# Merging two of the three products of a weight tile where there are 256 tokens

## The chip, the cores and the metric

The kernel runs on one core of a Trainium2 chip. TensorE (PE) multiplies, with its weight loader (PEld) beside it; VectorE (DVE), ScalarE (ACT) and GpSimd (POOL) do elementwise work; SyncE (SP) issues the loads of the weights. The metric is device time in microseconds for one execution. The kernel before took 2243.93 us, the median of three runs (2242.37 to 2246.74).

## The reference

A network in float32 over 256 tokens with 1024 features, preceded by 16 meta tokens (272 rows in all). The first block is a mixer (a state-space part and a conformer convolution, joined by one output product) and a mixture of experts; the second block has two layers, each a feed-forward part, an attention and a feed-forward part. The expert layer has 16384 experts with one row each; a token uses 16 of them for each of 8 heads:

```
h = h + concatenate([y_ssd, y_conf]) @ w_out
q = (xt @ w_query).reshape(t, 8, 256)
expert_idx, gate = top 16 of the sums of the two halves' scores
act = gelu(einsum("td,thkd->thk", xt, w_down[idx])) * gate
h = h + einsum("thk,thkd->td", act, w_up[idx])
...
ffn(x) = (silu(x @ wi_a) * (x @ wi_b)) @ wo
```

The meta tokens don't take part in the expert layer, and from the second layer's attention output on they are not needed either: there products have 256 columns, one per token, elsewhere mostly 272.

## The kernel before

Features stand on the partitions and tokens on the free axis. All large weights come in one stream, in the order of use, in chunks of eight 128x128 tiles. `_split` turns half a chunk (four tiles, 128x512) into two parts of TensorE's faster float32 type: ACT writes the first part H (L288, "wH"), then DVE or POOL the remainder L = w - H (L294, "wL"); the number `share` sets how many of the remainders go to POOL (0.5, every second one, in the down rows). The activations are cut in the same way, into uH and uL, cH and cL, gH and gL. `wtile` hands out a tile, and lets splits run up to four half chunks ahead.

`mm3` computes one tile of a product with three products into one PSUM bank: H by xH (L315), H by xL (L316), L by xH (L317). `linear` walks over the output tiles, each with its own bank (three "mm" banks at the expert layer), and calls `evac` with the sum; `linear_cut` interleaves the first few output tiles. `pair` does two outputs together, for the feed-forward part's input. All are used in every stage but one, the "up" product of the experts, which has a loop of its own (L999).

The stages with 256 columns that the change is about: the mixer's output product w_out (16 sums, L649, DVE adds each to h); the experts' query (16 tiles, L835 multiplies by the norm's factor, then the scores L840 and the search for the 16 best on DVE); the down product (`peer`, 128 rows of 8 tiles, each row 128 experts by 256 tokens, closed by a Gelu on ACT in `value`, L957); the second attention's output (`proj_out`); and the last feed-forward part's output (L1093).

All experts are computed, as a dense product, and the gates of those not chosen are zero. The gates are built beside the down product. The choice of experts (`route`, a generator) is issued in steps between the rows, `pace` 1.5 steps a row: its dense part runs over 128x864 elements in L894, L895 and L897 on DVE. From row 60 on the gates are made four tokens at a time: `onehot` (L931, L933 and, on ACT, L936) writes one-hot rows, `gates` turns them into gates with eight passes of TensorE (L943) and multiplies (L945). The order on each engine is the order in which the program was written down by the scheduler; an engine works it off in that order.

## Time and profile before

| | |
|---|---|
| median of three runs | 2243.93 us |
| span of the profiled execution | 2244.9 us |
| TensorE busy | 2174.1 us (97%), 17351 instructions |
| weight loader busy | 2100.5 us (94%) |
| VectorE busy | 1587.7 us (71%) |
| ScalarE busy | 1322.5 us (59%) |
| GpSimd busy | 672.5 us (30%) |
| traffic | 356.59 MB, 159 GB/s on average |

The profile is of one execution, and its own time is the span; little lies around it, as the run's first and last records are a load and a store. A "busy" matmul counts from its start to a modelled end, so that neighbouring ones overlap; distances between starts are the better measure. "a <- b" in a row of waits says that a waited for b. The stages on the timeline, by the first product of each: w_out 193.5 to 255 us, query to 308.4, down to 762 (its rows 60 to 127 from 508.7), up to 1128, the second block to the end, whose last stage, from about 2178 on, is the last feed-forward part's output.

### The profile page before, as it was taken

The page shows a single profiled execution, that of the slowest core. Times are in us where ns is not written, and L with a number is a line of the kernel's source. Part 1 is how long each engine was busy: PE and PEld are TensorE (multiplying, and loading weights), DVE is VectorE, ACT ScalarE, POOL GpSimd, SP SyncE. Part 2 cuts the span into 40 slices and gives each one's busy share as a digit, 9 for nine tenths or more (in the row PEclk, how much of TensorE's full clock was granted, in tenths as well). Part 3 has the DMA queues.
Part 4 walks back from the last instruction along what each step waited for, and adds up shares of the span by engine and source line. Part 5 has one row for each costly group of instructions (what it writes and reads, how often), then busy time and mean ns, then how long its engine had stood idle before and what let it go on. Part 6 is the DMA issues. An engine that isn't in the chain of part 4 may idle for free.

```text
span 2244.9 us, 45779 instructions
## 1 busy us (share of the span) xinstructions
PE 2174.1 (97%) x17351; PEld 2100.5 (94%) x17351; DVE 1587.7 (71%) x3143; ACT 1322.5 (59%) x2857; POOL 672.5 (30%) x567
## 2 busy tenths in 40 slices
PE   8998998899999999999999999999999999899999
PEld 7987997899999999999999998899999999679999
DVE  8899789946778765666586655876656666877664
ACT  8776654556766655555555555765555555656553
POOL 6685744444555300000031123122201212412220
PEclk9999999999999999999999999999999999999999
DMA  4534644454444555555565554145555555204554
GB/s 169 166 104 132 201 142 149 159 181 150 142 135 139 186 185 185 188 186 183 186 199 192 178 169 133 65 152 170 178 179 170 172 178 178 76 29 141 183 188 157
DMA packets 103948, 356.59 MB, mean 159 GB/s; under 512 B 12416, under 2 KB 20016, under 8 KB 103344
## 3 DMA queue, kind: packets, MB, share of 16 engines
q1 hardware_dynamic: 100096, 346.06, 46.6%
q10 hardware_dynamic: 3632, 7.62, 1.0%
q8 instruction: 136, 2.23, 0.4%
q14 instruction: 84, 0.69, 0.1%
HBM read 351.51 MB, written 5.40 MB: 159 GB/s over the span
## 4 chain that ended last, share of the span: by engine, by line
PE 77%; DVE 14%; ACT 4%; issue 3%; POOL 1%; DMA 1%; SPq 0%; DVEq 0%; ACTq 0%; POOLq 0%
PE acc L999 16%; PE mm L315 14%; PE mm L317 14%; PE mm L316 14%; PE acc L317 4%; PE acc L316 4%; PE acc L315 4%; DVE wL L294 3%; DVE h L931 2%; DVE acc L526 1%; ACT h L936 1%; PE acc L943 1%; PE mm L1458 1%; ACT wH L288 1%; PE acc L1482 1%
## 5 line engine op out<-in xcount | busy, mean ns | idle before, releaser
L288 ACT ACTIVATE wH<-raw 128x512 fp32r<-128x512 f32 x1296 | 806.3, 629 | 565.0 <-PE mm L316 251.5
L294 DVE TENSOR_TENSOR wL<-raw,wH 128x512 fp32r<-128x512 f32 x1037 | 757.1, 731 | 388.5 <-ACT wH L288 369.0
L317 PE MATMUL mm<-uH,wL 128*128 128x256 f32 (+1 forms) x2168 | 619.6, 286 | 21.8 <-DVE wL L294 20.8
L315 PE MATMUL mm<-uH,wH 128*128 128x256 f32 (+1 forms) x2168 | 627.6, 290 | 9.9 <-ACT wH L288 6.9
L316 PE MATMUL mm<-uL,wH 128*128 128x256 f32 (+1 forms) x2168 | 618.9, 285 | 2.2 <-DVE uL L359 2.0
L294 POOL TENSOR_TENSOR wL<-raw,wH 128x512 fp32r<-128x512 f32 x259 | 384.1, 1488 | 462.6 <-ACT wH L288 357.9
L317 PEld LDWEIGHTS mm<-uH,wL 128*128 128x128 f32 x2168 | 410.3, 189 | 27.1 <-DVE wL L294 26.2
L315 PEld LDWEIGHTS mm<-uH,wH 128*128 128x128 f32 x2168 | 410.3, 189 | 15.5 <-ACT wH L288 8.7
L316 PEld LDWEIGHTS mm<-uL,wH 128*128 128x128 f32 x2168 | 410.0, 189 | 5.7 <-DVE uL L359 4.0
L999 PE MATMUL acc<-uH,wH 128*128 128x256 f32 x1024 | 288.4, 282 | 2.7 <-ACT uH L355 1.6
L999 PE MATMUL acc<-uL,wH 128*128 128x256 f32 x1024 | 287.7, 281 | 0.4 <-DVE uL L357 0.4
L999 PE MATMUL acc<-uH,wL 128*128 128x256 f32 x1024 | 287.2, 281 | 0.0
L1083 POOL TENSOR_TENSOR t<-t,g 128x272 f32<-128x272 f32 (+1 forms) x88 | 108.4, 1233 | 416.7 <-ACT wH L288 320.5
L317 PE MATMUL acc<-uH,wL 128*128 128x272 f32 (+1 forms) x728 | 209.3, 288 | 0.0
L316 PE MATMUL acc<-uL,wH 128*128 128x272 f32 (+1 forms) x728 | 209.0, 287 | 0.0
L315 PE MATMUL acc<-uH,wH 128*128 128x272 f32 (+1 forms) x728 | 208.9, 287 | 0.0
L315 PE MATMUL mm<-gH,wH 128*128 128x272 f32 (+1 forms) x704 | 201.9, 287 | 0.0
L317 PE MATMUL mm<-gH,wL 128*128 128x272 f32 (+1 forms) x704 | 201.7, 286 | 0.0
L316 PE MATMUL mm<-gL,wH 128*128 128x272 f32 (+1 forms) x704 | 201.5, 286 | 0.0
L999 PEld LDWEIGHTS acc<-uH,wH 128*128 128x128 f32 x1024 | 194.1, 190 | 3.4 <-ACT uH L355 1.8
L999 PEld LDWEIGHTS acc<-uL,wH 128*128 128x128 f32 x1024 | 193.1, 189 | 0.6 <-DVE uL L357 0.6
L999 PEld LDWEIGHTS acc<-uH,wL 128*128 128x128 f32 x1024 | 193.1, 189 | 0.0
(400 smaller groups left out, 3914.1 us busy)
## 6 DMA issues: line engine op xcount, KB each, us to landing
raw<-in_wall_dram SPq DMA_DIRECT2D x648, 512.0 KB, 3.3
bdram<-brow ACTq DMA_DIRECT2D x1, 3200.0 KB, 13.9
b<-bdram SPq DMA_DIRECT2D x8, 272.0 KB, 5.3
b<-bdram SPq DMA_DIRECT2D x8, 144.0 KB, 3.7
buf<-in_keys_dram ACTq DMA_DIRECT2D x1, 1024.0 KB, 7.1
hd<-h ACTq DMA_DIRECT2D x1, 1024.0 KB, 5.3
h<-hd ACTq DMA_DIRECT2D x1, 1024.0 KB, 7.5
uv<-in_uv_dram ACTq DMA_DIRECT2D x1, 1024.0 KB, 5.9
```

Source lines behind the costliest of these rows:

```text
L288: nc.scalar.activation(out=H, in_=w, func=AF.Copy)
L294: eng.tensor_tensor(out=L, in0=w, in1=H.bitcast(F32), op=ALU.subtract)
L315: mm(ps, H, xH, start=(k == 0), stop=False)
L316: mm(ps, H, xL, start=False, stop=False)
L317: mm(ps, L, xH, start=False, stop=(k == kt - 1))
L526: nc.vector.scalar_tensor_tensor(out=acc, in0=src, scalar=w, in1=acc, op0=ALU.mult, op1=ALU.add)
L931: nc.vector.tensor_tensor(out=o, in0=self.iota[:, None, None, :].to_broadcast([P, 4, 2, P]), in1=sel[:, ts, :, None].to_broadcast([P, 4, 2 ...
L936: nc.scalar.activation(out=o[:, t, 0], in_=o[:, t, 0], func=AF.Copy, scale=gsel[:, 4 * g + t : 4 * g + t + 1])
L943: nc.tensor.matmul(ps[:, :, t], o[:, t, 1], o[:, t, 0], start=True, stop=True)
L999: nc.tensor.matmul(o, a, b, start=(r == 0 and d % 2 == 0 and i == 0), stop=(r == NT - 1 and i == 2), skip_group_check=True)
L1083: nc.gpsimd.tensor_tensor(out=t, in0=t, in1=s, op=ALU.mult)
L1458: nc.tensor.matmul(ps[:, :nk], qa[hh][:, k, a : a + n], ckv[:, k, :nk], start=(k == 0), stop=(k == 1))
```

## The change

Both parts of the rows are kept in one tile, [partition, feature block, part, token]: uu, nn, cc, gg, oo, qp. Where a product has 256 tokens and is called with `wide=True`, its result takes a full bank as two halves of 256: H meets both parts in one 512-column product (first half xH, second half xL), and L meets xH in a 256-column product into the first half. The halves are added afterwards. `add_to` (w_out, the second attention's output) adds both halves to h, one after the other on DVE. `whole` (query, down rows) copies one half to SBUF on ACT and adds the other on DVE. The last feed-forward part's output does its scaled sum twice. The up product and all 272-column products keep three products a tile.

```diff
-        self.uH = per.tile([P, KD, T], F32R, name="uH")
-        self.uL = per.tile([P, KD, T], F32R, name="uL")
+        self.uu = per.tile([P, KD, 2, T], F32R, name="uu")
+        self.uH, self.uL = self.uu[:, :, 0], self.uu[:, :, 1]
...
     def mm3(self, ps, x, kt, a=0, b=None):
         mm = self.nc.tensor.matmul
         for k in range(a, kt if b is None else b):
             H, L = self.wtile()
-            xH, xL = x(k)
-            mm(ps, H, xH, start=(k == 0), stop=False)
-            mm(ps, H, xL, start=False, stop=False)
-            mm(ps, L, xH, start=False, stop=(k == kt - 1))
+            xx = x(k)
+            if len(ps.shape) == 3:
+                mm(ps, H, xx, start=(k == 0), stop=False)
+                mm(ps[:, 0], L, xx[:, 0], start=False, stop=(k == kt - 1))
+            else:
+                mm(ps, H, xx[:, 0], start=(k == 0), stop=False)
+                mm(ps, H, xx[:, 1], start=False, stop=False)
+                mm(ps, L, xx[:, 0], start=False, stop=(k == kt - 1))
...
+    def result(self, n, wide, tag="mm"):
+        ps = self.bank(tag)
+        return ps.rearrange("p (w n) -> p w n", w=2) if wide else ps[:, :n]
+    def linear(self, mt, kt, x, n, evac, tags=("mm",), wide=False):
         for m in range(mt):
-            ps = self.bank(tags[m % len(tags)])[:, :n]
+            ps = self.result(n, wide, tags[m % len(tags)])
             self.mm3(ps, x, kt)
             self.flush()
             evac(m, ps)
 
-    def linear_cut(self, mt, kt, at, x, n, evac):
-        ps = [self.bank()[:, :n] for _ in range(CUT)]
+    def linear_cut(self, mt, kt, at, x, n, evac, wide=False):
+        ps = [self.result(n, wide) for _ in range(CUT)]
         for m in range(CUT):
             self.mm3(ps[m], x, kt, 0, at)
         for m in range(CUT):
             self.mm3(ps[m], x, kt, at, kt)
             evac(m, ps[m])
-        self.linear(mt - CUT, kt, x, n, lambda m, p: evac(m + CUT, p))
+        self.linear(mt - CUT, kt, x, n, lambda m, p: evac(m + CUT, p), wide=wide)
+    def add_to(self, o, ps):
+        for i in range(2):
+            self.nc.vector.tensor_tensor(out=o, in0=ps[:, i], in1=o, op=ALU.add)
+    def whole(self, ps):
+        t = self.t_("sq", 3)[:, :S]
+        self.nc.scalar.activation(out=t, in_=ps[:, 1], func=AF.Copy)
+        self.nc.vector.tensor_tensor(out=t, in0=ps[:, 0], in1=t, op=ALU.add)
+        return t
 
...
-        return lambda k: (self.uH[:, k, a:b], self.uL[:, k, a:b])
+        return lambda k: self.uu[:, k, :, a:b]
...
-            cH = pool.tile([P, KD, S], F32R, name="cH")
-            cL = pool.tile([P, KD, S], F32R, name="cL")
+            cc = pool.tile([P, KD, 2, S], F32R, name="cc")
+            cH, cL = cc[:, :, 0], cc[:, :, 1]
...
-                nc.vector.tensor_tensor(out=h[:, m, M:], in0=ps, in1=h[:, m, M:], op=ALU.add)
-            self.linear_cut(8, KD, 4, lambda k: (yH[:, k], yL[:, k]), S, add)
+                self.add_to(h[:, m, M:], ps)
+            self.linear_cut(8, KD, 4, self.u(M, T), S, add, wide=True)
...
-            self.linear(8, KD, lambda k: (cH[:, k], cL[:, k]), S, add2)
+            self.linear(8, KD, lambda k: cc[:, k], S, add2, wide=True)
...
-                nc.vector.tensor_tensor(out=q, in0=ps, in1=r, op=ALU.mult)
+                nc.vector.tensor_tensor(out=q, in0=self.whole(ps), in1=r, op=ALU.mult)
...
-            self.linear(16, KD, self.u(M, T), S, qf)
+            self.linear(16, KD, self.u(M, T), S, qf, wide=True)
...
             def value(r, ps):
                 n = 4 * done
+                ps = self.whole(ps)
                 if n < S:
...
-                self.linear(1, KD, self.u(M, T), S, lambda m, ps: value(r_, ps))
+                self.linear(1, KD, self.u(M, T), S, lambda m, ps: value(r_, ps), wide=True)
...
-            gH = pool.tile([P, KF, n], F32R, name="gH")
-            gL = pool.tile([P, KF, n], F32R, name="gL")
+            gg = pool.tile([P, KF, 2, n], F32R, name="gg")
+            gH, gL = gg[:, :, 0], gg[:, :, 1]
...
-                nc.vector.scalar_tensor_tensor(out=self.h[:, m, lo:], in0=ps, scalar=0.5, in1=self.h[:, m, lo:], op0=ALU.mult, op1=ALU.add)
+                for p in (ps[:, 0], ps[:, 1]) if lo else (ps,):
+                    nc.vector.scalar_tensor_tensor(out=self.h[:, m, lo:], in0=p, scalar=0.5, in1=self.h[:, m, lo:], op0=ALU.mult, op1=ALU.add)
...
-            self.linear(8, KF, lambda k: (gH[:, k], gL[:, k]), n, add)
-    def proj_out(self, oH, oL, nxt, lo=0):
+            self.linear(8, KF, lambda k: gg[:, k], n, add, wide=lo > 0)
...
         self.norm_begin(nxt, lo)
 
         def add(m, ps):
-            self.nc.vector.tensor_tensor(out=self.h[:, m, lo:], in0=ps, in1=self.h[:, m, lo:], op=ALU.add)
+            if lo:
+                self.add_to(self.h[:, m, lo:], ps)
+            else:
+                self.nc.vector.tensor_tensor(out=self.h[:, m], in0=ps, in1=self.h[:, m], op=ALU.add)
             self.norm_tile(m)
 
-        self.linear_cut(8, KD, 6, lambda k: (oH[:, k], oL[:, k]), T - lo, add)
+        self.linear_cut(8, KD, 6, lambda k: oo[:, k], T - lo, add, wide=lo > 0)
```

On TensorE, in a late row of the down product (banks mm, halves of chunks wH and wL, the gates' acc), before:

```order
L943 MATMUL acc_8501<-h_77 128x128 x4
L315 MATMUL mm_8510<-uH_78,wH_8430 128x256
L316 MATMUL mm_8510<-uL_79,wH_8430 128x256
L317 MATMUL mm_8510<-uH_78,wL_8431 128x256
L315 MATMUL mm_8510<-uH_78,wH_8430 128x256
L316 MATMUL mm_8510<-uL_79,wH_8430 128x256
L317 MATMUL mm_8510<-uH_78,wL_8431 128x256
L315 MATMUL mm_8510<-uH_78,wH_8430 128x256
L316 MATMUL mm_8510<-uL_79,wH_8430 128x256
L317 MATMUL mm_8510<-uH_78,wL_8431 128x256
```

and of the change:

```order
L965 MATMUL acc_6939<-h_77 128x128 x4
L318 MATMUL mm_6951<-uu_78,wH_6877 128x512
L319 MATMUL mm_6951<-uu_78,wL_6878 128x256
L318 MATMUL mm_6951<-uu_78,wH_6877 128x512
L319 MATMUL mm_6951<-uu_78,wL_6878 128x256
L318 MATMUL mm_6951<-uu_78,wH_6877 128x512
L319 MATMUL mm_6951<-uu_78,wL_6878 128x256
L318 MATMUL mm_6951<-uu_78,wH_6877 128x512
L319 MATMUL mm_6951<-uu_78,wL_6878 128x256
L318 MATMUL mm_6951<-uu_78,wH_6908 128x512
```

A weight tile has two rows now, and the row of experts keeps its place beside the gates' products.

On DVE, the last part of the routing's dense steps (buf) between the splits of the weights (wL), before:

```order
L897 TENSOR_REDUCE buf<-buf 128x16
L894 TENSOR_TENSOR buf<-buf,cst 128x864
L294 TENSOR_TENSOR wL<-raw,wH 128x512
L895 TENSOR_TENSOR buf<-buf 128x864
L894 TENSOR_TENSOR buf<-buf,cst 128x864
L897 TENSOR_REDUCE buf<-buf 128x16
L294 TENSOR_TENSOR wL<-raw,wH 128x512
L895 TENSOR_TENSOR buf<-buf 128x864
L894 TENSOR_TENSOR buf<-buf,cst 128x864
L294 TENSOR_TENSOR wL<-raw,wH 128x512
L897 TENSOR_REDUCE buf<-buf 128x16
L895 TENSOR_TENSOR buf<-buf 128x864
```

and of the change, where L916, L917 and L919 are the three lines that were L894, L895 and L897:

```order
L363 TENSOR_TENSOR sq<-mm,sq 128x256
L294 TENSOR_TENSOR wL<-raw,wH 128x512
L919 TENSOR_REDUCE buf<-buf 128x16
L294 TENSOR_TENSOR wL<-raw,wH 128x512
L363 TENSOR_TENSOR sq<-mm,sq 128x256
L916 TENSOR_TENSOR buf<-buf,cst 128x864 x2
L294 TENSOR_TENSOR wL<-raw,wH 128x512
L363 TENSOR_TENSOR sq<-mm,sq 128x256
L917 TENSOR_TENSOR buf<-buf 128x864 x2
L363 TENSOR_TENSOR sq<-mm,sq 128x256
L294 TENSOR_TENSOR wL<-raw,wH 128x512
L919 TENSOR_REDUCE buf<-buf 128x16 x2
```

The sum of the two halves (L363) comes once per row, and the same three lines stand among more splits than before.

On DVE, where the gates begin (one-hots h, gates' product acc, values buf), before:

```order
L294 TENSOR_TENSOR wL_6449<-raw_6430,wH_6448 128x512
L294 TENSOR_TENSOR wL_6485<-raw_6466,wH_6484 128x512
L294 TENSOR_TENSOR wL_6523<-raw_6504,wH_6522 128x512
L294 TENSOR_TENSOR wL_6571<-raw_6552,wH_6570 128x512
L945 TENSOR_TENSOR buf_3273<-acc_6539,buf_3273 128x62x4
L931 TENSOR_TENSOR h_77<-cst_68,sel_3275 128x1024
L961 TENSOR_TENSOR buf_3273<-t_6587,buf_3273 128x4
L945 TENSOR_TENSOR buf_3273<-acc_6590,buf_3273 128x63x4
L294 TENSOR_TENSOR wL_6622<-raw_6603,wH_6621 128x512
L931 TENSOR_TENSOR h_77<-cst_68,sel_3275 128x1024
L945 TENSOR_TENSOR buf_3273<-acc_6641,buf_3273 128x64x4
```

and of the change (L953 was L931, L967 was L945, L984 was L961):

```order
L294 TENSOR_TENSOR wL_6062<-raw_6047,wH_6061 128x512
L363 TENSOR_TENSOR sq_6030<-mm_6003,sq_6030 128x256
L953 TENSOR_TENSOR h_77<-cst_68,sel_3160 128x1024
L967 TENSOR_TENSOR buf_3158<-acc_6034,buf_3158 128x62x4
L363 TENSOR_TENSOR sq_6073<-mm_6046,sq_6073 128x256
L953 TENSOR_TENSOR h_77<-cst_68,sel_3160 128x1024
L984 TENSOR_TENSOR buf_3158<-t_6077,buf_3158 128x4
L967 TENSOR_TENSOR buf_3158<-acc_6080,buf_3158 128x63x4
L294 TENSOR_TENSOR wL_6108<-raw_6093,wH_6107 128x512
L363 TENSOR_TENSOR sq_6119<-mm_6092,sq_6119 128x256
L953 TENSOR_TENSOR h_77<-cst_68,sel_3160 128x1024
L967 TENSOR_TENSOR buf_3158<-acc_6126,buf_3158 128x64x4
```

One sum per row stands between the one-hots, the gates' multiplication and the splits.

## Rows read from the trace of the kernel before

**Rows 1.** The page: span, busy times, chain by engine and line, a costly group
```profile
span 2244.9 us, 45779 instructions
...
PE 2174.1 (97%) x17351; PEld 2100.5 (94%) x17351; DVE 1587.7 (71%) x3143; ACT 1322.5 (59%) x2857; POOL 672.5 (30%) x567
...
PE 77%; DVE 14%; ACT 4%; issue 3%; POOL 1%; DMA 1%; SPq 0%; DVEq 0%; ACTq 0%; POOLq 0%
PE acc L999 16%; PE mm L315 14%; PE mm L317 14%; PE mm L316 14%; PE acc L317 4%; PE acc L316 4%; PE acc L315 4%; DVE wL L294 3%; DVE h L931 2%; DVE acc L526 1%; ACT h L936 1%; PE acc L943 1%; PE mm L1458 1%; ACT wH L288 1%; PE acc L1482 1%
...
L294 DVE TENSOR_TENSOR wL<-raw,wH 128x512 fp32r<-128x512 f32 x1037 | 757.1, 731 | 388.5 <-ACT wH L288 369.0
```

**Rows 2.** Windows: stretch, length, busy us of PE, PEld, DVE, ACT, POOL; PEclk
```profile
193.50:230.00 36.50, 34.22 (x240) 30.38 (x238) 31.50 (x65) 24.39 (x52) 16.14 (x14) 1.00 0.34 112
255.00:308.40 53.40, 52.77 (x447) 52.57 (x447) 42.11 (x140) 27.31 (x53) 32.70 (x26) 1.00 0.64 210
308.40:463.00 154.60, 132.22 (x1066) 127.23 (x1066) 151.06 (x432) 75.34 (x149) 67.99 (x45) 1.00 0.45 147
463.00:508.70 45.70, 45.70 (x389) 45.70 (x388) 13.48 (x19) 24.32 (x48) 20.81 (x17) 1.00 0.59 191
508.70:657.00 148.30, 148.30 (x1273) 148.30 (x1272) 103.93 (x143) 101.53 (x305) 75.19 (x58) 1.00 0.42 141
657.00:762.00 105.00, 103.46 (x875) 102.40 (x874) 82.01 (x100) 67.37 (x215) 56.75 (x42) 1.00 0.47 153
```

**Rows 3.** PE's waits, 308.4 to 463 us: total us, times, longest
```profile
PE mm L317 <- DVE wL L294: 20.0, 19, 3.0
```

**Rows 4.** DVE's groups, 308.4 to 463 us: busy us, mean ns, idle before
```profile
L294 DVE TENSOR_TENSOR wL<-raw,wH 128x512 fp32r<-128x512 f32 x44 | 42.8, 976 | 2.2 <-ACT wH L288 2.2
```

**Rows 5.** Windows, PE alone: stretch, length, busy (instructions under way), PEclk
```profile
466.00:500.00 34.00, 34.00 (x290) 1.00 0.59 193
1500.00:1600.00 100.00, 100.00 (x795) 1.00 0.53 175
```

**Rows 6.** Timeline of PE, two streams: start us, us, instruction
```profile
252.72 0.28 PE L315 MATMUL mm<-cH,wH 128*128 128x256 f32 x1
...
253.63 0.28 PE L317 MATMUL mm<-cH,wL 128*128 128x256 f32 x1
...
2237.77 0.28 PE L317 MATMUL mm<-gH,wL 128*128 128x256 f32 x1
...
2241.01 0.28 PE L317 MATMUL mm<-gH,wL 128*128 128x256 f32 x1
```

**Rows 7.** Line L1450: ns min/median/max, first and last start us
```profile
L1450 PE MATMUL mm<-uv,ckv x24: 591/592/592, 1946.4 to 1956.3; 128*72 128x512 f32 x16, 128*128 128x512 f32 x8
```

**Rows 8.** Timeline of DVE around one sum of w_out
```profile
208.01 0.42 DVE L649 TENSOR_TENSOR h<-mm,h 128x256 f32<-128x256 f32 x1 [0.20 <-PE mm L317]
208.35 1.01 DVE L526 SCALAR_TENSOR_TENSOR acc<-cin,vecs,acc 128x256 f32<-128x256 f32 x2
```

**Rows 9.** ACT's groups, 465 to 505 us
```profile
L957 ACT ACTIVATE buf<-mm 128x256 f32<-128x256 f32 x14 | 5.1, 365 | 0.0
```

**Rows 10.** Timeline: query's start, first down rows, the end; [idle before <-releaser]
```profile
255.32 0.35 PE L315 MATMUL mm<-uH,wH 128*128 128x256 f32 x1 [1.41 <-DVE h L649]
...
311.13 0.39 PE L315 MATMUL mm<-uH,wH 128*128 128x256 f32 x1 [0.67 <-ACT uH L355]
...
2241.69 0.42 DVE L1093 SCALAR_TENSOR_TENSOR h<-mm,h 128x256 f32<-128x256 f32 x1 [5.96 <-PE mm L317]
```

**Rows 11.** PE's waits, 508.7 to 762 us
```profile
PE acc L943 <- DVE h L933: 0.2, 1, 0.2
```

**Rows 12.** DVE's groups, 657 to 745 us
```profile
L931 DVE TENSOR_TENSOR h<-cst,sel 128x1024 f32<-128x1024 f32 x24 | 31.2, 1299 | 0.0
```

**Rows 13.** L316's loads, 465 to 505 and 1500 to 1600 us: ns min/median/max
```profile
L316 PEld LDWEIGHTS mm<-uL,wH x112: 187/188/192, 465.1 to 504.8; 128*128 128x128 f32 x112
...
L316 PEld LDWEIGHTS mm<-uL,wH x136: 188/188/189, 1499.9 to 1599.4; 128*128 128x128 f32 x136
```

More of the change, by code (lines that the diff above doesn't have):

```diff
@@ L326, in flush @@
                 f()
-    def linear(self, mt, kt, x, n, evac, tags=("mm",)):
+    def result(self, n, wide, tag="mm"):
+        ps = self.bank(tag)
+        return ps.rearrange("p (w n) -> p w n", w=2) if wide else ps[:, :n]
+    def linear(self, mt, kt, x, n, evac, tags=("mm",), wide=False):
         for m in range(mt):
-            ps = self.bank(tags[m % len(tags)])[:, :n]
+            ps = self.result(n, wide, tags[m % len(tags)])
             self.mm3(ps, x, kt)
@@ L466, in mixer @@
             NU = 2
-            nH = pool.tile([P, KD, T], F32R, name="nH")
-            nL = pool.tile([P, KD, T], F32R, name="nL")
-            un = lambda a=0, b=T: lambda k: (nH[:, k, a:b], nL[:, k, a:b])
+            nn = pool.tile([P, KD, 2, T], F32R, name="nn")
+            nH, nL = nn[:, :, 0], nn[:, :, 1]
+            un = lambda a=0, b=T: lambda k: nn[:, k, :, a:b]
             r = None
@@ L1097, in add, with proj_out @@
                     nc.sync.dma_start(out=self.out[:, m], in_=self.h[:, m, M:])
-            self.linear(8, KF, lambda k: (gH[:, k], gL[:, k]), n, add)
-    def proj_out(self, oH, oL, nxt, lo=0):
+            self.linear(8, KF, lambda k: gg[:, k], n, add, wide=lo > 0)
+    def proj_out(self, oo, nxt, lo=0):
         self.norm_begin(nxt, lo)
         def add(m, ps):
-            self.nc.vector.tensor_tensor(out=self.h[:, m, lo:], in0=ps, in1=self.h[:, m, lo:], op=ALU.add)
+            if lo:
+                self.add_to(self.h[:, m, lo:], ps)
+            else:
+                self.nc.vector.tensor_tensor(out=self.h[:, m], in0=ps, in1=self.h[:, m], op=ALU.add)
             self.norm_tile(m)
-        self.linear_cut(8, KD, 6, lambda k: (oH[:, k], oL[:, k]), T - lo, add)
+        self.linear_cut(8, KD, 6, lambda k: oo[:, k], T - lo, add, wide=lo > 0)
     QT = ((0, M, M), (M, P, 144), (144, P, T))
@@ L1205, in attn_a @@
             rq = self.token_root(pool, pq, 16, 1.0 / 64, 0.125)
-            oH = pool.tile([P, 8, T], F32R, name="oH")
-            oL = pool.tile([P, 8, T], F32R, name="oL")
+            oo = pool.tile([P, 8, 2, T], F32R, name="oo")
+            oH, oL = oo[:, :, 0], oo[:, :, 1]
             def tail(items):
@@ L1285, in attn_a @@
                     tail([(1, 6, 2), (2, 6, 2)])
-            self.proj_out(oH, oL, nxt)
+            self.proj_out(oo, nxt)
     def meta_p(self, pool, qq, kz, rq, nlam):
@@ L1326, in attn_b @@
             cq = pool.tile([P, 2, T], F32, name="cq")
-            qH = pool.tile([P, 2, T], F32R, name="qH")
-            qL = pool.tile([P, 2, T], F32R, name="qL")
+            qp = pool.tile([P, 2, 2, T], F32R, name="qp")
+            qH, qL = qp[:, :, 0], qp[:, :, 1]
             kix = pool.tile([P, 2, T], F32, name="kix")
@@ L1332, in attn_b @@
             vt = pool.tile([P, 3, 1024], F32, name="vt")
-            oH = pool.tile([P, 8, S], F32R, name="oH")
-            oL = pool.tile([P, 8, S], F32R, name="oL")
+            oo = pool.tile([P, 8, 2, S], F32R, name="oo")
+            oH, oL = oo[:, :, 0], oo[:, :, 1]
             r = None
@@ L1386, in qif @@
                 nc.scalar.activation(out=qi[:, m], in_=ps, func=AF.Copy)
-            cqx = lambda k: (qH[:, k], qL[:, k])
+            cqx = lambda k: qp[:, k]
             self.linear(4, 2, cqx, T, qif)
@@ L1504, in attn_b @@
                 rq = rnext
-            self.proj_out(oH, oL, nxt, M)
+            self.proj_out(oo, nxt, M)
     def second(self):
```

## The prediction

> **What bounds the kernel now.** I read the page first. The profiled execution spans 2244.9 us, its TensorE (PE) is busy 97%, its weight loader 94%, VectorE (DVE) 71% [rows 1]. Busy PE is no proof that PE is the bound, so the chain of work that ended last comes second: PE holds 77% of it, DVE 14%, and among its lines stand the three products of a weight tile with 14% each and, with 3% DVE's split of the weights (L294) [rows 1]. So the matmul stream sets most of the time, and somewhere DVE does. The busy times by stage, third, say where. From 308.4 to 463 us, the first part of the experts' down product, DVE is busy 151.06 of 154.6 us and PE 132.22; the waits of that stretch are PE for DVE's split, 20.0 us in 19 waits [rows 2, 3]. There DVE is the bound. From 463 to 508.7 and to 657 PE is busy all of the time, DVE 13.48 of 45.7 and 103.93 of 148.3 us; to 657–762 DVE has 82.01 of 105 [rows 2]. In the query (255 to 308.4) PE has 52.77 of 53.4 us.
>
> **The price of a product.** Today a 128x128 weight tile costs three 256-column products. Between 466 and 500 us 290 of them are under way in 34.0 us without a gap, two of them from before its start, so 118 ns each; with 272 columns it is 795 in 100 us, 126 ns [rows 5]. The clock granted there is full (1.00), 2.4 GHz, at which a column takes 0.417 ns, if one goes in per cycle: 256 columns 106.7 ns. So each product carries some 11 ns more than its columns. How much depends on the tile that is read: with cH and cL eight products take 252.72 to 253.63, 114 ns each; with gH and gL 27 take 2237.77 to 2241.01, 120 ns [rows 6]. Both have 256 columns. An extra that is 7 ns with one tile and 13 with another, at one count of columns, looks like something paid where a product starts on its rows rather than a rate per column. Against this: 126 over 118 is 1.07 and 272 over 256 is 1.0625, which a rate per column gives too. I can't exclude it.
>
> No 512-column product of this number type is in the trace. Bounds from the nearest rows, per weight tile, of now 355 ns (3 x 118.3):
> - The extra goes with the columns: 512 columns cost two of 256, the tile stays at 355 ns, gain 0.
> - The extra is paid once per product: one of three goes, gain 11.6 ns.
> - The extra vanishes in a long product: the plain fp32 passes of L1450, also 512 columns, start 24 times from 1946.4 to 1956.3 us, 23 intervals of 430 ns; two cycles a column would be 426.7 [rows 7]. With as little as that, some 3 ns, a product would take 216, the tile 216 + 118, gain 20.8 ns.
> - Below nothing: a jump inside a product, from the first part's row to the second's, could cost as much as a start and something more; the spread of 114 to 120 between tiles puts that at 3 ns per tile, a loss.
>
> I take the second, 11.6 ns.
>
> **The change part by part.** 1520 weight tiles merge two products into one: 128 of w_out, 128 of the query, 1024 of the 128 down rows, 64 of the second attention's output, 176 of the last feed-forward part. The 272-column products and the "up" stage (L999) stay. But 384 of the 1024 tiles stand in the 48 down rows where DVE is the bound; PE's gain is lost there. That leaves 1136 x 11.6 ns = 13.2 us off the path.
>
> What is added, in the order of the program:
> - w_out, 16 tiles: a second DVE add each. DVE's add from PSUM with 128x256 takes 0.42 us and the next starts 0.34 after it [rows 8]. DVE is busy 31.50 of 36.5 us in 193.5 to 230 [rows 2]; 8 x 0.34 = 2.7 us if none of it is covered, 0 if the 5 idle us take it. I take 1. At the turn to the query PE waits 1.41 us for this very add (255.32) [rows 10]: +0.34.
> - Query, 16 tiles: ACT copies one half (0.365 us, by L957, the same shape out of PSUM [rows 9]), DVE adds. Both have room (DVE 42.11 of 53.4). +0.5, for 0 to 1. At its end PE waits for uL's sources (311.13) [rows 10]; copy and add stand ahead, 0.37 + 0.34 = 0.7.
> - Down rows under DVE's bound. One would charge 48 adds x 0.34 = 16 us. The order on DVE says otherwise: the steps of the routing (three passes over 128x864) are issued at a set pace, and between the last query row and the last of these steps stood 41 splits of the weights; now 48 splits and 47 adds. The DVE-bound stretch is thus 7 rows longer. A split takes DVE 0.98 us there [rows 4], of which I count 0.9, since the next instruction starts before the end as after the add. The stretch's end moves by 7 x 0.9 + 47 x 0.34 = 22.3 us, from 463 to some 485. But these are not lost: at 463 16 rows stood before row 60 (45.7 us of 24 x 118.3 ns, 2.84 us a row), and at 485 there are nine. The seven rows are worth 19.9 us, so row 60 starts 2.4 us later. I take +2, from -1 to +6, and 16 if the spread covers nothing.
> - Down rows 60 to 127, with the gates. PE waits 0.2 us in all of 508.7 to 762 [rows 11]. A row takes 24 products and 8 of the gates, 3.73 us; DVE fills 70% of the stretch to 657 and 78% of the one after. An add per row of 0.34 to 0.42 us makes this about 80 and 89%. The add also stands, on an engine that works in order, between the one-hots (1.3 us each after 657 [rows 12]) and a bank's release, which so far ACT's Gelu gave; behind the add wait the next splits, and for these PE. Three result banks and splits two rows ahead cover it. I take +1.5, from 0 to 6.
> - attn_b's output: 0, PE doesn't wait at its end. Last feed-forward part: DVE is idle 5.96 us before the last sum [rows 10]; only the last tile's second operation stands between the last product and the store: +0.4.
>
> Costs: 1 + 0.34 + 0.5 + 0.7 + 2 + 1.5 + 0.4 = 6.4 us. Sum: 2244.9 - 13.2 + 6.4 = 2238.1 for the profiled execution; its span is 1.0 us over the median of 2243.93, so the forecast is 2243.93 - 6.8 = **2237.1 us**.
>
> The Trainium skill ("TensorE: Matmul & The Clock Gate", Back-to-back issue gap) states for a single product N/2.4 + 2.5 ns when warm, and adds that sustained streams of 512 columns ran at about 131 ns. The formula gives 109 ns for 256 columns, and the rows here show 114 to 120, so it misses what this stream pays; for 512 columns it gives 216 ns, by which the third bound above, some 2227 us, would come out.
>
> **The rivals.**
> - *A product costs by its columns.* The gain is 0 and the costs stay: 2243.93 + 6.4 = 2250.3. For it: the ratio of 272 to 256 columns; and a wide product reads two rows with a jump between, so a start may be paid twice. Against: the 114 and 120 ns at equal width.
> - *The extra vanishes.* 1136 x 20.8 = 23.6 us: 2243.9 - 23.6 + 6.4 = 2226.7. For it: the fp32 products. Against: those run at half the rate and may hide a start.
> - *The weight loads set the pace.* The loader is busy 94%, and a third of the loads goes: the tile comes down to its 768 columns, 320 ns, 1136 x 35 = 39.8 us, 2210.5. Against: the load takes 188 ns with 256 as with 272 columns, yet the products stand 118 and 126 ns apart [rows 5, 13]. The Trainium skill ("Perfetto Trace Analysis", Identifying the Most-Contended Engine) prefers the loader's busy share to the matmul's as a measure of how close a kernel is to its limit; by it this rival would be the likeliest.
> - *DVE becomes the bound of the late down rows* (the slow side). The place is rows 60 to 127, the price each row's full add, 0.34 us x 68 = 23 us less the 1.5 already charged: 2237.1 + 21.6 = 2258.7. It decides from the point where DVE's work per row exceeds 3.6 us; the shares give 2.6 to 2.9 now and 3.0 to 3.3 with the add, so it needs the one-hots' 1.3 us to come in bunches that the banks don't cover. For it: DVE's times swing with what runs beside, a split from 0.73 us over the program to 0.98 in the early rows [rows 1, 4]. Against: 0.2 us of waits now.
>
> **How the numbers follow.** Forecast 0.44, by columns 0.22, vanishes 0.14, loads 0.05, late rows 0.15. A measurement of this kernel tells 0.2%, 4.5 us, from no change: the bounds are 2239.4 and 2248.4. The likeliest case has its own range of 2231 to 2243 (costs from 2 to 12 us) and is faster in two thirds of it; by columns it is slower in six of ten; the two next are faster, the last slower. Faster 0.30 + 0.01 + 0.19 = 0.50; slower 0.13 + 0.13 = 0.26; same 0.24. The range of 2222 to 2256 leaves out the loads case, half of the late rows' and the ends of the others.
>
> **What would show it.** Right: in the query and between the routing's end and row 60 two product starts per tile, some 225 and 118 ns apart, 343 together; in the early down rows PE still waiting for L294, and its last such wait near 485 us; rows 60 on at 8 x 343 + 8 x 112 ns = 3.64 us with few waits. Wrong: a tile at 355 or at 334 ns; row 60 starting 10 us later than at 508.7; rows after it at 3.9 us or more with PE waiting for the add or for L294.

## The result, and the profile after

The changed kernel takes 2273.38 us (median of four runs, 2271.79 to 2275.13) against 2245.34 us for the kernel before (2242.37 to 2247.76): 1.0111 times as long, with a 95% interval of 1.0096 to 1.0126. The forecast was 2237.1 us, the range 2222 to 2256. The change costs 28 us where 7 us of gain were expected.

The page of the changed kernel: span, busy times, the chain by engine and by line, against [rows 1].

```profile
span 2273.3 us, 43211 instructions
...
PE 2183.8 (96%) x15831; PEld 2030.1 (89%) x15831; DVE 1671.1 (74%) x3319; ACT 1369.4 (60%) x3001; POOL 651.6 (29%) x567
...
PE 76%; DVE 15%; ACT 4%; issue 3%; POOL 1%; DMA 1%; SPq 0%; ACTq 0%; DVEq 0%; POOLq 0%
PE acc L1022 16%; PE mm L321 9%; PE mm L323 9%; PE mm L322 9%; PE mm L318 9%; PE mm L319 5%; PE acc L322 4%; PE acc L321 4%; PE acc L323 4%; DVE wL L294 4%; PE acc L965 1%; DVE acc L548 1%; PE mm L1485 1%; DVE h L953 1%; PE acc L1509 1%
```

The weight loader's share fell from 94 to 89%, the merge did what it says, and the span grew by 28.4 us. PE's busy time did not fall but rose, from 2174.1 to 2183.8 us, with 1520 instructions fewer. The chain gives no new culprit, so the stages have to be laid side by side. The starts of products at the borders of the stages give these differences ("end of the up product" is its last product):

| place | before | after | difference so far |
|---|---|---|---|
| w_out | 193.5 | 197.6 | +4.1 |
| query | 255.3 | 263.3 | +8.0 |
| first down row | 308.4 | 318.8 | +10.4 |
| first gates (row 61) | 514.4 | 529.9 | +15.5 |
| last gates | 752.0 | 783.6 | +31.6 |
| up | 762.4 | 792.3 | +29.9 |
| end of the up product | 1129.6 | 1157.5 | +27.9 |
| last feed-forward output | 2178.1 | 2208.4 | +30.3 |
| end | 2244.9 | 2273.3 | +28.4 |

More than half of the loss, 16.1 us, stands between the first and the last gates. Here are the gates' passes before and after: duration min/median/max in ns, then the first and the last start.

```profile
L943 PE MATMUL acc<-h x512: 272/275/377, 514.4 to 752.0; 128*128 128x128 f32 x171
```

```profile
L965 PE MATMUL acc<-h x512: 273/275/377, 529.9 to 783.6; 128*128 128x128 f32 x171
```

From 514.4 to 752.0 it was 237.6 us, now it is 253.7. The busy times of the stages after, in the columns of [rows 2] (w_out's first part, query, early down rows, counted from 320.4, where PE goes on after a pause in the first row, and two parts of the rows with gates):

```profile
197.60:236.30 38.70, 33.83 (x175) 26.73 (x173) 34.64 (x77) 26.73 (x58) 16.59 (x13) 1.00 0.30 102
263.30:320.40 57.10, 54.97 (x322) 48.12 (x322) 47.65 (x155) 31.20 (x70) 30.35 (x24) 0.97 0.55 186
320.40:478.00 157.60, 135.38 (x715) 109.11 (x716) 157.45 (x455) 85.66 (x191) 65.40 (x44) 1.00 0.44 144
529.90:600.00 70.10, 69.27 (x453) 62.60 (x452) 57.03 (x83) 53.64 (x160) 29.42 (x27) 1.00 0.40 134
600.00:783.60 183.60, 172.11 (x1071) 150.17 (x1070) 158.05 (x214) 131.61 (x406) 80.75 (x67) 1.00 0.39 129
```

Before, PE was busy in nearly all of these late rows [rows 2]; after 600 us it now has 172.11 of 183.6, with DVE at 158.05, or 86%. The waits of PE in the early rows (first fence) and between the first and last gates (second), against [rows 3, 11]:

```profile
PE mm L318 <- DVE sq L363: 14.4, 19, 1.0
PE mm L319 <- DVE wL L294: 4.4, 7, 1.0
```

```profile
PE acc L965 <- DVE h L955: 9.4, 12, 1.4
PE acc L965 <- ACT h L958: 2.3, 10, 0.3
```

In the early rows PE waited for DVE's split; now it waits for the sum, which frees the bank, and for the split together, about as long as before. In the late rows, where it waited 0.2 us, PE waits 11.7 us for the two engines that scale the one-hots by the gate: DVE (L955, every fourth group) and ACT (L958, the other groups). A matmul's end is modelled, so that part of a pause hides in PE's busy time. The weight loader's waits for the same two, between the same gates, are longer:

```profile
PEld acc L965 <- DVE h L955: 13.2, 12, 1.7
PEld acc L965 <- ACT h L958: 6.6, 19, 0.5
```

The price of the merged product can be read from the timeline of PE, in a down row (uu), in w_out's second part (cc) and in the last part (gg):

```profile
531.10 0.39 PE L318 MATMUL mm<-uu,wH 128*128 128x512 f32 x1
...
533.20 0.40 PE L318 MATMUL mm<-uu,wH 128*128 128x512 f32 x1
...
244.84 0.40 PE L318 MATMUL mm<-cc,wH 128*128 128x512 f32 x1
...
249.79 0.40 PE L318 MATMUL mm<-cc,wH 128*128 128x512 f32 x1
...
2219.86 0.39 PE L318 MATMUL mm<-gg,wH 128*128 128x512 f32 x1
...
2231.99 0.39 PE L318 MATMUL mm<-gg,wH 128*128 128x512 f32 x1
```

Six tiles of uu take 2.10 us, 350 ns each, where three products took 355. Fourteen tiles of cc take 4.95 us, 354 ns, where it was 3 x 114 = 341 [rows 6]: a loss. Thirty-five tiles of gg take 12.13 us, 347 ns, where it was 3 x 120 = 360: a gain of 13. The 512-column product alone stands 0.23 us (230 to 235 ns in the mean of each stage) ahead of the next, 17 to 22 ns above its columns' 213.3.

### The profile page after: what moved, and what is told of

The parts are those of the page before. It is cut to its first block, busy times and chain, and to the rows that moved or that the text cites. A ratio compares the mean times of both kernels' runs of the same rounds, so it can differ in the third digit from the quotient of the medians.

```text
span 2273.3 us, 43211 instructions
## 1 busy us (share of the span) xinstructions
PE 2183.8 (96%) x15831; PEld 2030.1 (89%) x15831; DVE 1671.1 (74%) x3319; ACT 1369.4 (60%) x3001; POOL 651.6 (29%) x567
## 4 chain that ended last, share of the span: by engine, by line
PE 76%; DVE 15%; ACT 4%; issue 3%; POOL 1%; DMA 1%; SPq 0%; ACTq 0%; DVEq 0%; POOLq 0%
PE acc L1022 16%; PE mm L321 9%; PE mm L323 9%; PE mm L322 9%; PE mm L318 9%; PE mm L319 5%; PE acc L322 4%; PE acc L321 4%; PE acc L323 4%; DVE wL L294 4%; PE acc L965 1%; DVE acc L548 1%; PE mm L1485 1%; DVE h L953 1%; PE acc L1509 1%
## 5 line engine op out<-in xcount | busy, mean ns | idle before, releaser
L318 PE MATMUL mm<-uu,wH 128*128 128x512 f32 x1216 | 442.5, 404 | 19.4 <-DVE sq L363 15.0
L1022 PE MATMUL acc<-uu,wH 128*128 128x256 f32 x2048 | 362.8, 281 | 1.4 <-DVE h L1056 1.0
L319 PE MATMUL mm<-uu,wL 128*128 128x256 f32 x1216 | 345.4, 284 | 6.8 <-DVE wL L294 5.0
L1022 PEld LDWEIGHTS acc<-uu,wH 128*128 128x128 f32 x2048 | 313.6, 188 | 2.5 <-DVE h L1056 1.4
L318 PEld LDWEIGHTS mm<-uu,wH 128*128 128x128 f32 x1216 | 229.5, 189 | 75.6 <-DVE sq L363 20.3
L1022 PE MATMUL acc<-uu,wL 128*128 128x256 f32 x1024 | 287.1, 281 | 0.0
L321 PE MATMUL mm<-uu,wH 128*128 128x272 f32 (+1 forms) x952 | 278.6, 293 | 8.3 <-ACT wH L288 7.3
L322 PE MATMUL mm<-uu,wH 128*128 128x272 f32 (+1 forms) x952 | 277.2, 291 | 2.1 <-DVE uu L381 2.1
L323 PE MATMUL mm<-uu,wL 128*128 128x272 f32 (+1 forms) x952 | 276.0, 290 | 1.3 <-DVE wL L294 1.2
L319 PEld LDWEIGHTS mm<-uu,wL 128*128 128x128 f32 x1216 | 230.5, 190 | 14.1 <-DVE wL L294 11.3
L322 PE MATMUL acc<-uu,wH 128*128 128x272 f32 (+1 forms) x728 | 209.3, 288 | 0.0
L321 PE MATMUL acc<-uu,wH 128*128 128x272 f32 (+1 forms) x728 | 208.6, 286 | 0.0
L321 PEld LDWEIGHTS mm<-uu,wH 128*128 128x128 f32 x952 | 181.1, 190 | 12.6 <-ACT wH L288 7.4
L322 PEld LDWEIGHTS mm<-uu,wH 128*128 128x128 f32 x952 | 182.0, 191 | 4.4 <-DVE uu L381 4.0
L323 PEld LDWEIGHTS mm<-uu,wL 128*128 128x128 f32 x952 | 181.0, 190 | 2.0 <-DVE wL L294 2.0
```

Source lines behind the costliest of these rows:

```text
L318: mm(ps, H, xx, start=(k == 0), stop=False)
L319: mm(ps[:, 0], L, xx[:, 0], start=False, stop=(k == kt - 1))
L321: mm(ps, H, xx[:, 0], start=(k == 0), stop=False)
L322: mm(ps, H, xx[:, 1], start=False, stop=False)
L323: mm(ps, L, xx[:, 0], start=False, stop=(k == kt - 1))
L1022: nc.tensor.matmul(o, a, b, start=(r == 0 and d % 2 == 0 and i == 0), stop=(r == NT - 1 and i == 2), skip_group_check=True)
```

## The experiments

**Is it the adds or the merged product?** Four kernels, run together; the kernel before stood at 2246.5 us beside them. The first drops the second half of each result.

```diff
 def whole(self, ps):
-    t = self.t_("sq", 3)[:, :S]
-    self.nc.scalar.activation(out=t, in_=ps[:, 1], func=AF.Copy)
-    self.nc.vector.tensor_tensor(out=t, in0=ps[:, 0], in1=t, op=ALU.add)
-    return t
+    return ps[:, 0]
... (and in add_to and the last feed-forward part)
```

> The changed kernel with the merged products, but the second half of each result (H by xL) is left out of the sum: no copy on ACT, no added operation on DVE. Theory (the loss is the adds: their place on DVE in the down rows, and the pauses they make at the turns of the stages): 2236 to 2246 us, since a merged tile takes 350 instead of 355 ns in the down rows and nothing is added; the gates' stretch of the down rows (first to last gate) comes back from 253.7 to 235 to 238 us. Rival (the merged product itself costs: it holds banks and weights longer, or the thinner weight loading lets the clock fall): 2262 us or more, the gates' stretch at 250 us or more.

2236.98 us, ratio 0.9958 (0.9945 to 0.9972); the gates' stretch is 233.0 us (515.1 to 748.1). The theory holds: the merge itself, with the rows in one tile, is worth 9.5 us, 6.3 ns for each of 1520 tiles, and the adds cost the 36 us between this and the changed kernel. The second keeps the adds and splits the merged product again.

```diff
-                mm(ps, H, xx, start=(k == 0), stop=False)
+                mm(ps[:, 0], H, xx[:, 0], start=(k == 0), stop=False, skip_group_check=True)
+                mm(ps[:, 1], H, xx[:, 1], start=False, stop=False, skip_group_check=True)
...
```

> The changed kernel with its two halves and all its adds, but H meets xH and xL in two 256-column products again. Theory (the adds cost): as slow as the changed kernel or a little slower, 2270 to 2282 us, the merged product being worth some 5 ns a tile, 1136 tiles, 6 us at most. Rival (the merged product costs): 2245 to 2256 us.

2282.09 us, ratio 1.0154 (1.0133 to 1.0176), 8.7 us above the changed kernel (7.6 if each is set against the kernel before beside it). From the other side it gives about the same worth of the merge. Third and fourth, the down rows, all of them or those from 60 on, go back to three products and to a value without the sum:

```diff
-                self.linear(1, KD, self.u(M, T), S, lambda m, ps: value(r_, ps), wide=True)
+                self.linear(1, KD, self.u(M, T), S, lambda m, ps: value(r_, ps), wide=False)   # third
+                self.linear(1, KD, self.u(M, T), S, lambda m, ps: value(r_, ps), wide=r_ < 60) # fourth
... (and in value: no sum in these rows)
```

> The changed kernel with the down rows as before (three products, one result, no add); w_out, query, the second attention's output and the last feed-forward part stay merged. Theory (most of the loss stands in the down rows): 2249 to 2257 us, with the gates' stretch at 237 to 239 us. Rival (the loss comes from the turns of the stages and the clock's falls there): 2262 us or more.

> The changed kernel with down rows 60 to 127 (those beside the gates) as before, rows 0 to 59 merged. Theory (the add holds up DVE's one-hots in these rows): the gates' stretch at 237 to 239 us instead of 253.7, in all 2254 to 2261 us. Rival (that stretch is long because the work of the earlier rows was pushed into it, or because of the clock): 2268 us or more.

2249.08 us (ratio 1.0012, 1.0001 to 1.0022) and 2257.23 us (1.0053, 1.0032 to 1.0073). So of the loss some 16 us are the late down rows, 8 us the early ones (by the difference of these two medians; in the trace of the changed kernel the way from the first down row to the first gates is 5.1 us longer than before, and 6.3 longer than in the third kernel, 318.5 to 523.3), and 3 us are left for the rest, where the last part gives back 1.9.

**What in the late rows?** My first theory was that DVE's occupied time paces them, as the slow rival had it. Four kernels, beside which the kernel before stood at 2249.87 us: the sum on GpSimd behind two copies of ACT; three of four splits on GpSimd, in the late rows or in all down rows; and a version that was to profit by it.

```diff
-        self.nc.vector.tensor_tensor(out=t, in0=ps[:, 0], in1=t, op=ALU.add)
+        self.nc.scalar.activation(out=o, in_=ps[:, 0], func=AF.Copy)
+        self.nc.gpsimd.tensor_tensor(out=t, in0=o, in1=t, op=ALU.add)
... (another kernel)
             for r_ in range(NT):
+                self.share = 0.75 if r_ >= 60 else 0.5
```

> The changed kernel with the sum of the two halves in the query and the down rows taken off DVE: ACT copies both halves (0.37 us each) and GpSimd adds them; the other added sums stay. Theory (DVE's occupied time per row, adds and the wait for ACT's copy together, paces the rows beside the gates): the stretch from the first to the last gate comes down from 253.7 us to 236 to 241, and the whole to 2247 to 2258 us, unless GpSimd's splits of the weights come late by it. Rival (the chain from a row's end over copy and sum to the values and on to the next gates is what paces, on whatever engine it runs): the stretch stays at 250 us or more.

> The changed kernel with three of four weight splits on GpSimd instead of every second one, in the rows from 60 on; the sums stay on DVE. Theory (DVE's occupied time paces these rows; half a split less per row is some 0.4 us less of its 3.9): the stretch from the first to the last gate at 236 to 243 us instead of 253.7, the whole at 2256 to 2264. Rival (the chain over copy and sum paces): no change in the stretch, within 2 us; or GpSimd's slower splits become what PE waits for, and it gets longer.

> The same share of three in four splits on GpSimd, in all down rows. Theory: as the run before for the late rows; in the early rows, where the sums came on top of a DVE that already was the bound, some 48 half splits of 0.9 us less, at most 20 us, of which GpSimd's 1.4 us per split leave perhaps half: the first gate 5 to 12 us earlier than in the run before. Rival (GpSimd becomes the bound in the early rows, PE waits for its splits): the first gate as late or later.

> Merged products only where the sum is hidden: down rows 48 to 127 (with three of four splits on GpSimd from row 60) and the last feed-forward part; w_out, query, down rows 0 to 47 and the second attention's output as before. Theory: 80 rows at 8 tiles and 5 ns give back 3 us, the last part 2 us: 2238 to 2243 us, a little under the kernel before. Rival (the late rows are held up by the chain over copy and sum, whatever DVE's load): 2250 us or more.

They got slower: 2330.92 (1.0364, 1.0347 to 1.0381), 2289.64 (1.0183, 1.0166 to 1.0200), 2283.42 (1.0155, 1.0138 to 1.0172) and 2276.8 us (1.0122, 1.0106 to 1.0139). The gates' stretch went from 253.7 to 295.0, 269.8, 270.1 and 269.7 us. In the all-rows version the first gates came 5.3 us earlier than in the late-rows version (519.6 against 524.9), at the low end of what was expected. PE's wait with the sum on GpSimd, then with three of four splits there:

```profile
PE acc L966 <- DVE h L956: 35.0, 15, 2.8
```

```profile
PE acc L965 <- ACT h L958: 19.9, 23, 1.2
```

With three of four splits on GpSimd PE waits for ACT's scaling instead, 19.9 us. The groups of DVE between 600 and 733 us (busy us, mean ns, idle before), first in the changed kernel, then with more splits on GpSimd:

```profile
L953 DVE TENSOR_TENSOR h<-cst,sel 128x1024 f32<-128x1024 f32 x32 | 43.5, 1359 | 0.0
...
L363 DVE TENSOR_TENSOR sq<-mm,sq 128x256 f32<-128x256 f32 x32 | 13.5, 420 | 19.5 <-ACT sq L362 19.5
```

```profile
L953 DVE TENSOR_TENSOR h<-cst,sel 128x1024 f32<-128x1024 f32 x31 | 48.3, 1557 | 0.0
L363 DVE TENSOR_TENSOR sq<-mm,sq 128x256 f32<-128x256 f32 x31 | 13.1, 421 | 20.4 <-ACT sq L362 20.4
```

The one-hot (L953, two operands in SBUF) went from 1.36 to 1.56 us when GpSimd had more to do; the sum (L363, one operand in PSUM) stayed at 0.42. DVE's scaling (L955) went from 0.68 to 1.33 us. So DVE got back all that was taken from it: between the first and last gates it is busy 221.4 us, where the changed kernel has 215.1. The Trainium skill ("SBUF — State Buffer", Who interferes with whom) says that a DVE operation with two SBUF inputs contends with GpSimd's reads, and that one with at most one, outside its two-port modes, does not; these rows agree. With the sum on GpSimd DVE does have less to do, 199.8 us, but ACT has more, 200.3 instead of 185.3, and waits 65 us for the sum. These kernels thus don't show that DVE's load is without effect; they show that moving it in this way doesn't help. I looked for another cause in the trace of the changed kernel. Timeline of all engines around two groups of gates:

```profile
667.22 0.61 PE L965 MATMUL acc<-h 128*128 128x128 f32 x4
...
667.70 0.39 ACT L958 ACTIVATE h<-h,gsel 128x128 f32<-128x128 f32 x1
667.99 0.37 ACT L362 ACTIVATE sq<-mm 128x256 f32<-128x256 f32 x1
...
668.15 1.05 PE L965 MATMUL acc<-h 128*128 128x128 f32 x4 [0.32 <-ACT h L958]
...
668.26 0.40 ACT L958 ACTIVATE h<-h,gsel 128x128 f32<-128x128 f32 x1
...
670.34 1.76 DVE L294 TENSOR_TENSOR wL<-raw,wH 128x512 fp32r<-128x512 f32 x1
...
671.15 0.38 ACT L362 ACTIVATE sq<-mm 128x256 f32<-128x256 f32 x1
...
671.49 0.40 PE L318 MATMUL mm<-uu,wH 128*128 128x512 f32 x1
...
672.03 0.68 DVE L955 TENSOR_TENSOR h<-h,gsel 128x512 f32<-128x512 f32 x1
...
672.76 0.49 PE L965 MATMUL acc<-h 128*128 128x128 f32 x2 [0.76 <-DVE h L955]
```

In the first, ACT makes the third scaling at 667.70, then the copy of a row's half (L362), and only then the fourth scaling at 668.26. The gates' passes, which PE wants to do right behind a row's last product, start at 667.22 for two tokens and go on at 668.15. In the second, the scaling that DVE does stands behind a split of 1.76 us. So a new theory: order, not load. The copy, I thought, waits for the row's last product and holds up the scaling behind it. The order could be moved without touching the work:

```diff
-                self.linear(1, KD, self.u(M, T), S, lambda m, ps: value(r_, ps), wide=True)
+                def evac(m, ps):
+                    if ahead:                 # rows 61 on: the next one-hot before this row's value
+                        onehot(pend + 1)
+                    value(r_, ps)
...
+        with self.behind(self.nc.scalar) if late else ExitStack():
             self.nc.scalar.activation(out=t, in_=ps[:, 1], func=AF.Copy)
+        with self.behind(self.nc.vector) if late else ExitStack():
             self.nc.vector.tensor_tensor(out=t, in0=ps[:, 0], in1=t, op=ALU.add)
```

> The changed kernel, only the order moved in rows 61 to 127: ACT's four scalings of a one-hot by the gate come before the copy of the row's half (in the changed kernel the last one or two stand behind it). DVE's order is the same as in the changed kernel. Theory (the copy waits for the row's end on an engine that works in order, and the scalings behind it make PE wait in every fourth group of gates): that wait, about 0.85 us in 16 of the 64 groups, goes, 13 us or a little less: the stretch from the first to the last gate at 240 to 247 us instead of 253.7, the whole 2261 to 2267. Rival (DVE's and ACT's occupied time paces, the order does not matter): the stretch within 2 us of 253.7.

2257.4 us (beside 2246.34; ratio 1.0049, 1.0034 to 1.0063), the gates' stretch 238.2 us:

```profile
L967 PE MATMUL acc<-h x512: 273/275/377, 528.1 to 766.3; 128*128 128x128 f32 x171
```

That is more than expected (240 to 247): the wait for DVE's scaling shrank as well, from 9.4 to 2.4 us. Timeline and waits of this kernel:

```profile
668.12 0.98 ACT L960 ACTIVATE h<-h,gsel 128x128 f32<-128x128 f32 x3
...
669.00 0.37 ACT L363 ACTIVATE sq<-mm 128x256 f32<-128x256 f32 x1
...
669.53 1.05 PE L967 MATMUL acc<-h 128*128 128x128 f32 x8
```

```profile
PE acc L967 <- DVE h L957: 2.4, 7, 0.5
```

All scalings stand ahead of the copy, and the gates' eight passes run through. DVE and ACT are busy for as long as in the changed kernel (213.5 and 188.8 us between the first and last gates, 215.1 and 185.3 there), and DVE's order is the same; so it is ACT's order that gave the time back.

My picture of how was wrong. In the whole changed kernel ACT was idle before a copy once, for 0.3 us: the copy hardly ever waits for a product. The one at 671.15 above starts before the last H product of the row under way (671.49); it is that of the row before, whose last product ended at 667.4. These are the waits of ACT and DVE between the first and last gates of the changed kernel:

```profile
ACT buf L980 <- DVE sq L363: 31.7, 16, 2.2
ACT buf L969 <- DVE buf L967: 19.2, 30, 1.2
ACT h L958 <- DVE h L953: 15.7, 40, 0.8
```

```profile
DVE sq L363 <- ACT sq L362: 37.8, 42, 1.4
```

Each of the two waits for the other: DVE's sum for the copy, the one-hot stands behind the sum, ACT's scalings wait for the one-hot, and the next copy stands behind them. Put beside their rows in order, the copies start 0.5 us behind the row's last product at the first gates, 3.0 us a dozen rows later, and from there mostly 3 to 4 us. So a round of the two engines takes longer than PE's row, they fall behind by about a row, and then PE waits: up to 600 us it is idle for 0.8 us, after that for 11.5. With the scalings first the lag takes some 25 rows to reach 3 us. Which link of the round the order shortened was not tried. The next kernel gives ACT the remaining scaling too, and the one after merges only where it is hidden:

```diff
-                if g % 4 == 0:
+                if False:                     # all four scalings on ACT
...
+                self.linear(1, KD, self.u(M, T), S, evac, wide=r_ >= 48)   # the one after
```

> The run before, and the scaling of every fourth one-hot, which DVE did behind a split and a gates' product, given to ACT as well. Theory: the second wait of four groups, about 0.85 us in 16 groups, goes too, and DVE has 0.7 us less per four rows: the stretch at 234 to 240 us, the whole 2253 to 2260. Rival (ACT, with 1.4 us more per four rows, becomes what PE waits for): the stretch no shorter than in the run before.

> As the run before, but merged only in down rows 48 to 127 and in the last feed-forward part; w_out, query, down rows 0 to 47 and the second attention's output as in the kernel before. Theory: 640 tiles at 5 ns and 176 at 13 ns less, 5 us, and little paid for the sums: 2238 to 2246 us, the kernel before at 2245 to 2249 beside it. Rival (the sums in the late rows still cost more than the merge gives, on whatever order): 2250 us or more.

2253.57 us (1.0034, 1.0021 to 1.0047), a stretch of 233.0 us, in which PE has no wait and the copies keep 0.3 to 0.6 us behind their rows; and 2236.18 us (0.9948, 0.9931 to 0.9965), which beats both kernels by more than expected. The rows with gates of this last one, as busy times by window and as first and last start:

```profile
513.70:600.00 86.30, 86.30 (x566) 78.30 (x565) 59.90 (x105) 77.03 (x232) 45.97 (x35) 1.00 0.44 144
600.00:746.70 146.70, 146.70 (x957) 133.04 (x956) 125.62 (x178) 128.41 (x396) 79.05 (x60) 1.00 0.43 144
```

```profile
L967 PE MATMUL acc<-h x512: 273/275/275, 513.7 to 746.7; 128*128 128x128 f32 x171
```

PE is busy in all of it; ACT, at 205 of 233 us, is the next to be full. A last kernel takes the merge out of this version and leaves the layout and the scalings where they are:

```diff
-                self.linear(1, KD, self.u(M, T), S, evac, wide=r_ >= 48)
+                self.linear(1, KD, self.u(M, T), S, evac)
```

> The run before (the faster version) without any merged product: the same layout of the rows in one tile, the same place and engine for the scaling of the one-hots, but three products a tile everywhere and no added sums. Theory (the merge in rows 48 to 127 and in the last part is worth some 5 us): 2240 to 2246 us, the stretch from the first to the last gate at 235 to 238 us. Rival (the gain came from the scaling's place or the layout, the merge is worth nothing): as fast as the run before, 2234 to 2238 us, the stretch at 233.

2251.94 us, beside 2248.83 for the kernel before (ratio 1.0019, 1.0007 to 1.0031), with a stretch of 242.8 us. This is slower than either side expected. The rival falls: without the merge nothing is gained. But 16 us between the last two kernels (13 if each is set against the kernel before beside it) is more than the 4 us of 640 tiles and the 2 of the last part. Some of the rest is in the late rows, whose second half slows here, and where the weight loader waits for ACT's scalings 12 times; why, and why eleven of its twelve runs lie 3 to 9 us over its profiled one, was not tried.

## Why the prediction was wrong

- *Down rows 60 to 127, "+1.5, from 0 to 6".* This step failed. The adds there cost 16.1 us in the trace, and 21 if one counts from 233.0, which the same rows take with the merge and without the adds. A row took 4.03 us (253.7 / 63), past the 3.9 that I had named as a sign of being wrong. I had asked whether DVE had room for one more operation, and whether banks and splits led far enough, and had PE wait for the splits. ACT's copy stood in this term at nothing, and so did the waits of DVE and ACT for each other. These are what the runs showed: a round of copy, sum, one-hot and scaling between two engines, neither of them full, takes longer than a row, and PE ends up waiting for the scalings. The order alone, at the same work, gave back 15.5 of the 16.1 us; DVE's scaling given to ACT as well gave the last 5.2, down to the 233.0. The rival *DVE becomes the bound of the late down rows* had the place and nearly the price (2258.7), but not the cause: with the scalings first DVE is as busy as in the changed kernel, 213.5 of now 238.2 us, or 90%, and PE waits 2.4 us for it. How the order shortens the round stays open.
- *The price of a product, 11.6 ns a tile.* Mis-sized: 5 ns with uu, 13 with gg, minus 12 with cc and with the second attention's oo. For the 1136 tiles that I had counted this makes some 5 us, of which I had written 13.2; for all 1520 it makes 7, and by the experiments the merge is worth 7.6 to 9.5. The extra of a product over its columns is 17 to 22 ns at 512 columns and 7 to 13 at 256: from 13 to 17 with gg, from 11 to 19 with uu, from 7 to 22 with cc. So gg comes near a price per start, and cc loses more than I had allowed for at the worst. My reading, that 114 against 120 ns at equal width speaks for a price per start, did not hold; cc, the cheapest before, became the dearest. What sets the extra is not shown. The rule of the Trainium skill ("TensorE: Matmul & The Clock Gate", Back-to-back issue gap) would have had 216 ns; the runs show 230 to 235, so it misses this stream by more at 512 columns than at 256.
- *Down rows under DVE's bound, "+2, from -1 to +6".* Within the range, at its upper end: 5.1 us in the trace against the kernel before, 6.3 against the kernel with narrow down rows, since the routing spread over more rows, as the order had shown. By the medians it is some 8 us, with the rows to 60 in it.
- *w_out, query and their ends, 1 + 0.34 + 0.5 + 0.7.* It took 6.3 us more from w_out's first product to the first down row. PE's pauses grew, and after two of them the clock fell. Timeline of PE, at the turn from w_out's first part to its second and at the turn to the query, and the granted clock behind them (length, busy, PEclk):

```profile
236.27 0.50 PE L318 MATMUL mm<-cc,wH 128*128 128x512 f32 x1 [2.59 <-ACT wH L288]
...
263.32 0.47 PE L318 MATMUL mm<-uu,wH 128*128 128x512 f32 x1 [2.07 <-DVE h L357]
```

```profile
236.00:238.00 2.00, 1.42 (x4) 0.78 0.00 0
238.00:240.00 2.00, 2.00 (x9) 0.50 0.32 82
240.00:242.00 2.00, 2.00 (x11) 0.86 0.86 274
...
264.00:266.00 2.00, 2.00 (x9) 0.61 0.79 303
266.00:268.00 2.00, 2.00 (x8) 0.54 0.89 301
```

  A pause of 2.59 us, then one of 2.07, and the granted clock is down to half (1.2 GHz) for some 3.4 us behind each, 1.7 us lost twice; before, there was no pause at the first place, the one at the query was 1.41 us long, and the clock stayed full. I had priced the added operations alone; but the first pause is 2.11 us in the kernel without the adds too, and is absent where w_out isn't merged (the last two kernels). At the query's end the 0.7 did not come: PE waits 0.68 us there, 0.67 before.
- *Ahead of w_out, where nothing was priced*, 4.1 us: two falls of the clock of 1.7 us each, at 104 and 138 us, which the trace of before does not have. Both follow pauses of PE that were there before with about the same length (1.9 us at 102, 1.2 and 1.3 at 134 us). Some of the other kernels show them and some don't. What decides it stays open. Two more such falls that the trace of before doesn't have, at 1428 and 1940 us, stand in the stretch from the end of the up product to the last feed-forward output, which lost 2.4 us.
- *The last part, +0.4*: right, 0.5; by its tiles the stage was 2.3 us shorter, 1.9 in all.
- *The ends of the other rivals.* Weight loads do not set the pace: a third fewer, and a tile gained 5 ns.

## What to carry to other kernels

Before an operation is added on an engine that "has room", follow what hands work to it and what it hands work to. If two engines pass a row's work back and forth, count one round of that, in the order of each engine, against the time of a row: a load of 70% says nothing of it. Here four scalings moved ahead of one copy gave back 15.5 of the 16.1 us of the late rows, at the same load. And the price of a longer product should be measured in the stream at hand with the tiles at hand, before it carries a forecast.

## What the runs showed of the hardware

- A 512-column product of the faster float32 type costs 230 to 235 ns in a full stream, the two 256-column products that it replaces 228 (cc) to 240 (gg).
- After pauses of PE of 2.59 and 2.07 us the granted clock fell to half (1.2 GHz) and stood there for some 3.4 us each; a pause of 1.9 us at 102 us was followed by a fall in the changed kernel and not in the one before.
- DVE's one-hot, 1.21 us alone, takes 1.8 to 2.0 us when a split of GpSimd runs beside it; its mean went from 1.36 to 1.56 us with three of four splits there.
